# Loading every b tile as two halves on two DMA queues, in a batched matrix product on one Trainium2 core

## Chip, cores and metric

The kernel runs on one core of a Trainium2 chip. The metric is the device time of one execution in microseconds (us). Before the change three runs took 134.62, 134.85 and 134.93 us; their median is 134.85 us.

## The reference

1024 independent products of 64 x 64 matrices, in fp32:

```python
def setup_inputs():
    return {
        "a": np.random.randn(1024, 64, 64).astype(np.float32),
        "b": np.random.randn(1024, 64, 64).astype(np.float32),
    }

def reference(a, b):
    return np.matmul(a, b).astype(np.float32)
```

a, b and the result have 16.78 MB each, so 33.55 MB are read from HBM and 16.78 MB are written.

## The kernel before

**Tiles.** The batch is cut into 16 tiles of 64 matrices (index t) and 8 super-tiles of 128 (index s). One b tile is 1 MB in fp32, `[128 partitions, 16 groups, 128]`: a group is four matrices, and each partition takes two rows of one matrix, 512 B, from every group. One super-tile of a is 2 MB in four parts of 512 KB. GpSimd's queue loads three of them and casts them to bf16 on the way (`a_sb`), SyncE's queue loads the fourth in fp32 (`a_raw`). For the first super-tile all four parts come in fp32 on SyncE's and ScalarE's queues.

**Work on a tile.** VectorE regroups a super-tile into one bf16 tile (`regroup`, L108 and L111). TensorE transposes it (`transpose`, L120), two bf16 values taken as one fp32, and ScalarE copies the transposes out of PSUM (L123). VectorE spreads them into a block-diagonal operand (`spread`, four copies a tile, L133) and casts the b tile to bf16 (`cast`, L144; tile 0 is cast by ScalarE, tile 15 in quarters by both, L149 and L151). Then 64 matmuls (`multiply`, L189) and eight copies from PSUM into the fp32 output tile `o_sb` (L177): all eight on ScalarE for even tiles, six on ScalarE and two on VectorE for odd ones.

**Order.** The program is one straight sequence, and each engine and each DMA queue takes its own instructions in that order. At tile t the sequence is: spread and cast of tile t+1; the load of b tile t+3, whose buffer is that of tile t (three buffers); at some even tiles loads and transposes of a; the matmuls and evacuation of tile t; regrouping and transposes for a later super-tile; the store of tile t-1. Three super-tiles of a have buffers. The output has eight buffers, two of which also take the first super-tile of a.

**Queues.** A transfer is issued by an engine's instruction stream. SyncE does nothing but issue. ScalarE issues between its copies, so an issue takes its time, and one that waits holds the copies behind it. GpSimd issues the casting loads of a and the stores of tiles 0 to 13, 1 MB each (L166). The stores of the last two tiles go out in pieces on SyncE's and ScalarE's queues. In the profile q0 is GpSimd's queue, q1 SyncE's and q10 ScalarE's; 16 DMA engines serve all three.

**What the change touches.** `load_b` (L93 to L97) issues each b tile as one transfer, even tiles on SyncE's queue and odd ones on ScalarE's (L96). It is called three times ahead of the loop (L215, L216, L221) and once in each of the first 13 tiles (L235). Ahead of the loop, ScalarE has its two loads of a (L90) and a first copy that loads its table (L214) before these, and its two casts of the first super-tile (L105) after them.

Of the kernel before, what the change touches and what calls it, by code (L numbers as in the profile page):

```python
# [13 lines left out]
def kernel(  # L14
# [14 lines left out]
    nc = tc.nc  # L29
# [11 lines left out]
    b_v = b.rearrange("(t g h) (kp u) n -> t (h kp) g (u n)", h=4, g=16, u=2)  # L41
# [50 lines left out]

    def load_b(t):  # L93
        b_sb = b_pool.tile([128, 16, 128], fp32, name="b_sb")
        queue = nc.scalar if t % 2 else nc.sync
        queue.dma_start(out=b_sb[:], in_=b_v[t])  # L96
        b_tiles[t] = b_sb  # L97

    def regroup(s):
# [110 lines left out]
    with tc.manual_schedule():  # L210
        load_first_a()

        nc.vector.memset(warm[:, 0:1], 0.0)
        nc.scalar.copy(warm[:, 1:2], warm[:, 0:1])  # L214
        load_b(0)  # L215
        load_b(1)  # L216
        nc.vector.memset(bd_tiles[0][:], 0.0)  # L217
        make_identity(nc, identity)
        nc.gpsimd.memset(bd_tiles[1][:, 0], 0.0)
        load_a(1)  # L220
        load_b(2)  # L221
        nc.gpsimd.memset(bd_tiles[1][:, 1], 0.0)
        load_a(2)
# [63 lines left out]
```

## Time and profile before

| | |
|---|---|
| median of 3 runs (lowest to highest) | 134.85 us (134.62 to 134.93) |
| span of the profiled execution, first to last instruction | 133.4 us |
| median less that span | 1.4 us |
| busy: VectorE, ScalarE, TensorE, GpSimd | 94.6, 87.9, 64.4, 33.0 us |
| packets and MB: q0, q1, q10 | 6832 and 20.19, 7120 and 14.68, 5056 and 9.96 |
| HBM read and written | 33.55 and 16.78 MB |
| b loads, issue to landing | 14.8 to 25.2 us, median 16.8 |
| matmuls of tile 0 begin, of tile 15 end | 21.2 and 120.2 us |
| last store issued | 125.85 us |

The profile's execution has no time listed beside its span. The 1.4 us that the median of the timed runs lies above it is taken as what lies around the span.

Times in the views count from the start of the span. The page's slices cut the span into 40 equal parts, with the busy share in tenths. The DMA row is the mean busy share of the 16 DMA engines, and the row below it is what they moved in GB/s, a casting load counted by the bytes that it writes. The chain follows the work that ended last back from the last instruction. In a timeline the brackets hold the idle time of the engine before the instruction, and what ended it. A queue such as SPq or ACTq stands for the issuing instructions of SyncE or ScalarE.

### The profile page before, as it was taken

How to read it: one execution, taken by the hardware profiler on the slowest of the kernel's cores; microseconds unless marked ns; L12 is line 12 of the kernel's file. 1: busy time of each engine (PE TensorE's matmuls, PEld its weight loads, DVE VectorE, ACT ScalarE, POOL GpSimd, SP SyncE). 2: the span in 40 equal slices, each digit the busy share in tenths (PEclk: the TensorE clock that was granted, in tenths of full speed). 3: DMA queues.
4: the chain of work that ended last, by engine and by line, in shares of the span. 5: the costliest groups of instructions: out<-in, count | busy, mean ns of one | idle time of the engine just before them, and what ended most of it. 6: DMA issues, size and time to landing. Idle time of an engine off the chain costs nothing.

```text
span 133.4 us, 2837 instructions
## 1 busy us (share of the span) xinstructions
PE 64.4 (48%) x1152; PEld 61.1 (46%) x1152; DVE 94.6 (71%) x120; ACT 87.9 (66%) x161; POOL 33.0 (25%) x43
## 2 busy tenths in 40 slices
PE   0006406960089384289518970956197363970000
PEld 0006306950089274189418950945196363960000
DVE  5930399109998809995999699959999995987000
ACT  3225424999036998969595969696968969099600
POOL 8991000420090070341233021203020410300000
PEclk9999975797557999856985699599959955599555
DMA  3999999999999999999999999999999999999990
GB/s 77 371 329 311 307 311 281 284 306 325 327 312 401 316 320 333 399 384 397 311 281 375 406 389 351 304 316 390 394 396 387 396 392 391 402 405 398 382 319 18
DMA packets 19021, 45.01 MB, mean 337 GB/s; under 512 B 1088, under 2 KB 3136, under 8 KB 19008
## 3 DMA queue, kind: packets, MB, share of 16 engines
q0 software_dynamic: 6832, 20.19, 50.1%
q1 hardware_dynamic: 7120, 14.68, 30.4%
q10 hardware_dynamic: 5056, 9.96, 19.7%
q8 instruction: 9, 0.15, 0.4%
q14 instruction: 4, 0.03, 0.1%
HBM read 33.55 MB, written 16.78 MB: 377 GB/s over the span
## 4 chain that ended last, share of the span: by engine, by line
DMA 53%; DVE 15%; ACT 13%; PE 6%; issue 5%; SPq 2%; DVEq 0%; ACTq 0%
DMA b_sb<-in_b_dram 53%; ACT o_sb L177 9%; DVE at_bd L133 6%; PE o_ps L189 4%; DVE b_bf L144 4%; DVE o_sb L177 3%; PE at_ps L120 2%; ACT at_sb L123 2%; ACT b_bf L144 1%; SPq L90 1%; DVE a_bf L108 1%; SPq L96 1%; ACT b_bf L151 1%; DVE a_bf L111 0%; SPq L77 0%
## 5 line engine op out<-in xcount | busy, mean ns | idle before, releaser
L177 ACT COPY o_sb<-o_ps 64x512 f32<-64x512 f32 x106 | 61.5, 580 | 10.3 <-PE o_ps L189 9.0
L189 PEld LDWEIGHTS <-at_bd 128*128 128x128 bf16 x1024 | 42.3, 113 | 39.5 <-DVE b_bf L144 25.7
L189 PE MATMUL o_ps<-b_bf,at_bd 128*128 128x64 bf16 x960 | 42.6, 216 | 35.4 <-DVE b_bf L144 23.4
L133 DVE COPY at_bd<-at_sb 32x1024 f32<-32x1024 f32 x64 | 46.9, 733 | 14.1 <-ACT at_sb L123 11.8
L120 PE MATMUL at_ps<-identity,a_bf 128*128 128x128 f32 x128 | 21.2, 335 | 19.4 <-ACT a_bf L105 11.2
L166 POOL DMA_DIRECT2D out_dram<-o_sb x14 | 15.4, 1097 | 56.9 <-ACT at_sb L123 23.4
L120 PEld LDWEIGHTS at_ps<-identity,a_bf 128*128 128x128 f32 x128 | 19.3, 180 | 19.5 <-issue 19.5
L123 ACT COPY at_sb<-at_ps 128x512 f32<-128x512 f32 x32 | 17.5, 590 | 11.0 <-PE at_ps L120 7.8
L144 DVE CAST b_bf<-b_sb 128x2048 bf16<-128x2048 f32 x14 | 17.8, 1271 | 9.6 <-DMA b_sb<-in_b_dram 9.4
L73 POOL DMA_DIRECT2D a_sb<-in_a_dram x21 | 13.6, 662 | 26.4 <-DVE a_bf L108 19.4
L177 DVE COPY o_sb<-o_ps 64x512 f32<-64x512 f32 x14 | 9.7, 690 | 0.3
L108 DVE COPY a_bf<-a_sb 128x3072 bf16<-128x3072 bf16 x7 | 6.7, 950 | 0.0
L105 ACT CAST a_bf<-o_sb 128x1024 bf16<-128x1024 f32 x2 | 2.1, 1044 | 5.2 <-DMA o_sb<-in_a_dram 5.2
L111 DVE CAST a_bf<-a_raw 128x1024 bf16<-128x1024 f32 x7 | 4.8, 683 | 0.0
L144 ACT CAST b_bf<-b_sb 128x2048 bf16<-128x2048 f32 x1 | 1.9, 1900 | 3.9 <-DMA b_sb<-in_b_dram 3.9
L105 DVE CAST a_bf<-o_sb 128x1024 bf16<-128x1024 f32 x2 | 2.8, 1382 | 1.9 <-DMA o_sb<-in_a_dram 1.9
L217 DVE MEMSET at_bd<- 128x4096 f32 x1 | 3.5, 3472 | 0.8 <-issue 0.8
L177 DVE COPY o_sb<-at_ps 64x256 f32<-64x256 f32 x8 | 3.4, 422 | 0.5 <-PE at_ps L189 0.4
L151 ACT CAST b_bf<-b_sb 128x512 bf16<-128x512 f32 x2 | 1.1, 615 | 3.6 <-DMA b_sb<-in_b_dram 3.6
L177 ACT COPY o_sb<-at_ps 64x256 f32<-64x256 f32 x8 | 2.9, 366 | 0.1
L214 ACT ACT_TABLE_LOAD x1 | 1.3, 1283 | 2.3 <-issue 2.3
L189 PE MATMUL at_ps<-b_bf,at_bd 128*128 128x64 bf16 x64 | 2.0, 193 | 1.0 <-DVE at_bd L133 1.0
(12 smaller groups left out, 6.1 us busy)
## 6 DMA issues: line engine op xcount, KB each, us to landing
out_dram<-o_sb POOLq DMA_DIRECT2D x14, 1024.0 KB, 21.6
a_sb<-in_a_dram POOLq DMA_DIRECT2D x21, 256.0 KB, 16.4
a_raw<-in_a_dram SPq DMA_DIRECT2D x7, 512.0 KB, 18.7
o_sb<-in_a_dram SPq DMA_DIRECT2D x2, 512.0 KB, 5.9
o_sb<-in_a_dram ACTq DMA_DIRECT2D x2, 512.0 KB, 7.1
out_dram<-o_sb SPq DMA_DIRECT2D x2, 512.0 KB, 7.5
out_dram<-o_sb SPq DMA_DIRECT2D x2, 256.0 KB, 7.8
out_dram<-o_sb ACTq DMA_DIRECT2D x2, 256.0 KB, 5.5
```

The costliest lines, as they stand in the source:

```text
L73: nc.gpsimd.dma_start(out=a_sb[:, h, :, :].rearrange("p v k -> p (v k)"), in_=a_v[s, h], single_packet=True)
L105: copy(a_bf[:, :, h, :], a_sb[h].rearrange("p (v k) -> p v k", v=16))
L108: nc.vector.tensor_copy(a_bf[:, :, 0:3, :], cast_sb[:].rearrange("p h v k -> p v h k"))
L111: nc.vector.tensor_copy(a_bf[:, :, 3, :], raw[:])
L120: nc.tensor.transpose(at_ps[:, vo, :], a_cols[:, 4 * vo + 2 * j + wl, :], identity[:])
L123: nc.scalar.copy(at_tiles[s][:, j, :, wl, :, :], at_ps[:].rearrange("p vo (g mp) -> p g mp vo", mp=4),)
L133: nc.vector.tensor_copy(bd[rows, :, :, :, h, :].rearrange("p j g wl mo -> p j (g wl) mo"), at_tiles[t // 2][rows, :, half, :, :, :].rearrange(
L144: (nc.vector.tensor_copy if t else nc.scalar.copy)(b_bf[:], b_sb[:])
L166: store_queue(t, lo).dma_start(out=o_v[t, :, lo : lo + n, :], in_=o_sb[:, lo : lo + n].rearrange("p gh j wl n -> p (gh j wl n)"),)
L177: copies[2 * par + wl](dst, src)
L189: nc.tensor.matmul(o_ps[:, gl, g % 2, j, :], at_bd[:, j, g, :, u], b_bf[:, g, 64 * u : 64 * u + 64], start=(u == 0), stop=(u == 1),)
L217: nc.vector.memset(bd_tiles[0][:], 0.0)
```

## The change

Every b tile is loaded by two transfers, groups 0 to 7 on SyncE's queue and groups 8 to 15 on ScalarE's. The places in the program, the buffers and everything else stay.

```diff
     def load_b(t):
         b_sb = b_pool.tile([128, 16, 128], fp32, name="b_sb")
-        queue = nc.scalar if t % 2 else nc.sync
-        queue.dma_start(out=b_sb[:], in_=b_v[t])
+        nc.sync.dma_start(out=b_sb[:, 0:8, :], in_=b_v[t][:, 0:8, :])
+        nc.scalar.dma_start(out=b_sb[:, 8:16, :], in_=b_v[t][:, 8:16, :])
         b_tiles[t] = b_sb
```

## The prediction

> **What bounds the kernel now.** I read the page's slices, queues and chain first, then the windows, then the timelines of ScalarE and SyncE, then the packet records behind the DMA figures. The page first.
>
> ```profile
> DMA  3999999999999999999999999999999999999990
> GB/s 77 371 329 311 307 311 281 284 306 325 327 312 401 316 320 333 399 384 397 311 281 375 406 389 351 304 316 390 394 396 387 396 392 391 402 405 398 382 319 18
> ...
> q0 software_dynamic: 6832, 20.19, 50.1%
> q1 hardware_dynamic: 7120, 14.68, 30.4%
> q10 hardware_dynamic: 5056, 9.96, 19.7%
> ...
> DMA b_sb<-in_b_dram 53%; ACT o_sb L177 9%; DVE at_bd L133 6%; PE o_ps L189 4%; DVE b_bf L144 4%; DVE o_sb L177 3%; PE at_ps L120 2%; ACT at_sb L123 2%; ACT b_bf L144 1%; SPq L90 1%; DVE a_bf L108 1%; SPq L96 1%; ACT b_bf L151 1%; DVE a_bf L111 0%; SPq L77 0%
> ```
>
> The chain tempts: 53% of it is waiting for b tiles, the very transfers that the change touches. But the DMA row above it is full in every slice but the first and the last. The three queues (q0 is GpSimd's, q1 SyncE's, q10 ScalarE's) sum to 100.2% of the engines' time. A b tile takes 15 to 25 us to land because it shares a full pool, not because its own queue is slow. The page's GB/s count casting loads by what they write, half of what they read. Counted by what they read, the packet records give 398.8 GB/s on average from 4 to 128 us, and between 383 and 407 in every stretch of 4 us. So 49.45 of the 50.33 MB pass at one steady rate. What is left to win is the two ends.
>
> ```profile
> 4.00:20.00 16.00, 3.60 (x16) 3.38 (x17) 8.21 (x10) 5.15 (x7) 6.38 (x9) 0.94 1.07 329
> ...
> 100.00:116.00 16.00, 9.73 (x187) 9.13 (x186) 14.10 (x18) 11.47 (x22) 2.72 (x3) 0.71 1.03 393
> ...
> 124.00:128.00 4.00, 0.00 (x0) 0.00 (x0) 0.00 (x0) 1.76 (x5) 0.00 (x0) 0.50 1.07 379
> 128.00:129.00 1.00, 0.00 (x0) 0.00 (x0) 0.00 (x0) 0.00 (x0) 0.00 (x0) 0.50 1.04 362
> 129.00:130.00 1.00, 0.00 (x0) 0.00 (x0) 0.00 (x0) 0.00 (x0) 0.00 (x0) 0.50 0.64 223
> 130.00:131.00 1.00, 0.00 (x0) 0.00 (x0) 0.00 (x0) 0.00 (x0) 0.00 (x0) 0.50 0.17 58
> 131.00:132.00 1.00, 0.00 (x0) 0.00 (x0) 0.00 (x0) 0.00 (x0) 0.00 (x0) 0.50 0.05 17
> ```
>
> These are windows; the last two columns are the DMA share and GB/s, the columns before them PE, weight load, VectorE, ScalarE, GpSimd and the clock. The pool is full until 129 us and then runs out engine by engine until the last packet ends at 131.8. The 0.30 MB after 129 would take 0.8 us at 400 GB/s, so a perfectly even end would come 2.0 us earlier. That is the most that the order of the transfers can win at the end. VectorE is next: 14.1 us busy of 16 around 110 us.
>
> ```profile
> 19.29 1.90 ACT L144 CAST b_bf<-b_sb 128x2048 bf16<-128x2048 f32 x1 [3.87 <-DMA b_sb<-in_b_dram]
> ...
> 90.34 0.02 ACT L96 MOVE_SHAPE b_sb<-in_b_dram  x1 [0.52 <-DVE b_bf L144]
> 90.39 0.69 ACTq L96 DMA_DIRECT2D b_sb<-in_b_dram  x1
> 91.13 1.07 ACT L123 COPY at_sb<-at_ps 128x512 f32<-128x512 f32 x2 [0.77 <-issue]
> 92.09 4.74 ACT L177 COPY o_sb<-o_ps 64x512 f32<-64x512 f32 x8
> 97.81 3.55 ACT L177 COPY o_sb<-o_ps 64x512 f32<-64x512 f32 x6 [0.99 <-PE o_ps L189]
> ```
>
> This is ScalarE's timeline (start, length, what, idle time before it). An issue on this queue costs ScalarE 0.77 us, and it comes once per pair of tiles. Before an odd tile's evacuation ScalarE waits 0.99 us for the matmuls (1.27 to 1.38 in the neighbouring pairs).
>
> **The change part by part.** *Bytes and packets.* The bytes stay. Each half still has rows of 512 B, so I expect the same 2 KB packets: 512 per tile (85 ns each), as two times 256. There are 16 more transfers, 8 on each queue, and each leaves one 4-byte packet on every DMA engine. These last 22 ns on q1 and 9 ns on q10 (medians): 8 x 22 + 8 x 9 = 0.25 us per engine. The bounds are 0, since packets overlap (shares of 1.03 to 1.09), and 0.25; I take +0.1.
>
> *SyncE's issues.* It issues 16 halves for 8 tiles, and computes nothing. Its a_raw loads stand in the same order behind the b loads, with about the same bytes ahead.
>
> *ScalarE's issues.* 8 more. The price of one half is bounded by the 0.38 us of a 512-row store and the 0.77 above; I take 0.75, as its rows are of the b load's kind. 8 x 0.75 = 6.0 us in all. Two of them come at the start and six before the evacuations of the odd tiles 1 to 11. At tiles 5 to 11 they fall into the 0.99 to 1.38 us wait for the matmuls; at tiles 1 and 3 the evacuations follow their predecessors without a gap, so 1.5 us are uncovered, in a stretch where the pool is full. On the path that sets the end: 0. Without the cover each issue would delay the evacuations, then the stores, by 0.75 us.
>
> *Tile 0 comes earlier.* Tiles 0 and 1 now share the pool and land at 19.26 and 20.42. In the packet records the two had 534 packets through by 14.0 us, more than one tile. Halved on both queues, tile 0 lands near 14.9. ScalarE then casts it after its last at_sb copy (15.41), and the first matmul waits for the spread of tile 0, which ends at 15.45 + 4 x 0.71 = 18.3, instead of the cast at 21.2: up to 2.9 us earlier. Against this, SyncE shows what an issue behind a b tile can cost:
>
> ```profile
> 3.27 6.36 SPq L77 DMA_DIRECT2D a_raw<-in_a_dram  x1
> ...
> 10.85 11.30 SPq L77 DMA_DIRECT2D a_raw<-in_a_dram  x1
> ```
>
> The a_raw load behind tile 0 was held for 6.36 us, until 9.63, when 68 of the tile's 512 packets were through; the one behind tile 2 went when 70 were. So about 444 packets fit in a queue. ScalarE now issues halves of tiles 0, 1 and 2 ahead of its two casts of a (at 6.34 and 10.05): 512 packets stand before the third, which may be held until about 70 are through, near 10.7 (83 of tile 1 were at 11.0). Both casts would follow it (0.75 + 2 x 1.04), ending at 13.5 instead of 11.1, and the first matmul would still come at 20.7. So the computation starts 0.5 to 2.9 us earlier.
>
> *Where that goes.* Later, VectorE waits 9.4 us in five places for b tiles (4.0 of them at 50 us, for tile 4 behind three a_raw loads). A tile on two queues lands sooner, and these waits shrink. But the pool was full before, so earlier loads only push stores back, and the bill comes at the end: stores then stand queued while the last tiles are computed. The reserve is there. Tile 13's evacuation (109.7) reuses the buffer of tile 5, whose store landed at 96.3, so stores may slip 13 us.
>
> *Two load queues at once.* In stretches of 2 us with both load queues over 40 GB/s the pool moved 399.9 GB/s beside casting loads and 393.8 beside stores; with one of them 401.9 and 396.1. Both were active in 36 of 54. If the remaining third joined at 0.5% less: 0.005 x 0.33 x 124 = +0.2 us. The loads would end earlier in return: bounds 0 and, at the 1% that stretches of 1 us show, +0.4. I take +0.2.
>
> *The end.* Bounds 0 and -2.0. The first and the last DMA engine of one load land 2 to 3 us apart in the middle of the run too (47.41 and 50.09 for tile 4), so most of the uneven end stays; the last stores show 3.6 us (128.51 and 132.10). Only this excess of about 1 us can go, and I take -0.6.
>
> Sum: +0.1 + 0.2 - 0.6 = -0.3 us on a span of 133.4. The median of the runs is 1.4 us above that span, so 134.5.
>
> A rule of the Trainium skill speaks against the change. "DMA: Bandwidth & Descriptors", section Rules for kernel authors, says not to split a transfer into halves on two queues, as both run over the same 16 engines. Its section Anatomy of one DMA has a fixed 2.0 us per transfer; as an estimate by that page, 16 more would cost 32 us if nothing lay beside them. The rows here have the pool's share above 1.0 all along, so that fixed part lies beside other packets, and the sum by the rows stands.
>
> **The rivals.**
> - *ScalarE is held at its issues* (slower). As SyncE's a_raw was, a half issued behind unfinished halves can be held, and evacuations queue behind it. For: the holds of 6.36 and 11.30 us. Against: when tile 12 was issued (83.28), tile 10 had been moving since 76.3, so well over 68 packets were gone, and ScalarE's queue carries no a_raw. The eight completion counters are reused too: a GpSimd load waited 5.3 us for an unrelated store that had the same one. It decides once the last store issue (125.85) comes over 2 us later, as 1.48 MB, 3.7 us, are still queued then; beyond that the end moves one for one. Holds of 3 to 5 us past the cover: 135.5 to 138.
> - *The mix costs more* (slightly slower): 0.25 for the packets, 0.4 for the queues, no gain at the end, up to 0.3 more where SyncE's half waits for a_raw: 135.2 to 135.8.
> - *Nothing changes*: SyncE's queue moves 14.68 MB against 9.96, so the half there sets when a tile is complete, as late as before: 134.6 to 135.1.
> - *The end fills up* (faster): stores stand queued for all engines until the last moment, and the whole 2.0 us go, less 0 to 1.0 for the terms above: 132.9 to 133.9.
>
> **How the numbers follow.** What a measurement here can tell from no change is about 0.2%, 0.27 us. Forecast 0.40 (134.0 to 135.0; 0.26 of it faster, 0.14 same), end filled 0.12 (faster), nothing 0.10 (0.08 same, 0.02 slower), mix 0.15 (0.01 same, 0.14 slower), ScalarE held 0.23 (slower). Faster 0.38, same 0.23, slower 0.39. The range, 133.4 to 136.2, leaves out half of the filled end and half of the held case.
>
> **What would show it.** Right: q1 with 7248 packets and q10 with 5184 (128 more each, 16 engines by 8 transfers), with 14.68 and 9.96 MB as before; the DMA row full as before; the cast of tile 0 starting before 18 us; the 4.0 us wait for tile 4 shorter; the last matmul earlier than 118 us while the span moves by under 1 us. Wrong: a DMA slice below 9 in the middle, ScalarE's L96 issues lasting over 1 us, its wait for the matmuls replaced by waits at L96, or a rate below 395 GB/s.

## The result and the profile after

The changed kernel takes 147.63 us (median of four runs, 146.28 to 149.16), the kernel before 134.89 us beside it. The ratio is 1.0903, with a 95% interval of 1.0845 to 1.0962; the slowest run of the change, 149.16 us, counts as disturbed and is left out of the ratio. So the change is slower by 9%, and the forecast of 134.5 us with its range up to 136.2 was wrong. The profiled execution took 148.07 us, its span is 146.2 us.

The page of the changed kernel, in the rows that were shown of before:

```profile
DMA  3999999999999999999999999999999999997476
GB/s 87 386 272 231 235 232 282 332 324 308 319 255 382 272 261 400 382 277 273 391 366 263 303 350 350 382 344 356 339 373 306 382 374 298 374 351 273 152 260 215
DMA packets 43853, 45.01 MB, mean 308 GB/s; under 512 B 1344, under 2 KB 36160, under 8 KB 43840
...
q0 software_dynamic: 6832, 20.19, 45.5%
q1 hardware_dynamic: 19536, 14.68, 34.5%
q10 hardware_dynamic: 17472, 9.96, 23.6%
```

The bytes are the same to the last digit, but q1 has 19536 packets for 7120 and q10 17472 for 5056. The records say what they are: 32768 packets of 512 B, at a median of 27 ns, stand where 8192 packets of 2 KB at 85 ns stood. Four small ones take 108 ns. With their means (88 and 31 ns), the time that packets of b keep one DMA engine went from 45.2 to 62.7 us, while all other packets stayed at 89 to 90 us. The DMA row is still full for most of the span; a full row says that the engines have packets, not that they move 400 GB/s: from 4 to 124 us the packet records, with casting loads counted by what they read, give 399 GB/s before and 368 now.

Windows (last two columns: DMA share and GB/s), the first of the kernel before, the others of the changed kernel:

```profile
12.00:20.00 8.00, 2.80 (x14) 2.55 (x13) 4.36 (x7) 3.06 (x5) 0.00 (x0) 0.88 1.08 310
...
12.00:20.00 8.00, 0.00 (x0) 0.00 (x0) 0.00 (x0) 1.18 (x2) 0.00 (x0) 1.00 1.13 234
...
128.00:132.00 4.00, 3.29 (x63) 3.16 (x61) 3.04 (x5) 0.80 (x2) 1.20 (x1) 0.50 0.90 337
132.00:136.00 4.00, 2.20 (x43) 2.15 (x41) 2.14 (x5) 2.57 (x5) 0.15 (x1) 0.50 0.81 279
136.00:140.00 4.00, 1.62 (x31) 1.46 (x28) 3.33 (x8) 3.89 (x8) 0.00 (x0) 0.50 0.39 131
140.00:146.20 6.20, 0.00 (x0) 0.00 (x0) 0.00 (x0) 2.24 (x7) 0.00 (x0) 0.50 0.76 254
```

From 12 to 20 us the changed kernel moves 234 GB/s for 310 at a share of 1.13 for 1.08, and has no matmul yet. A part of this drop is only that more of its bytes are casting loads: counted by what they read it is 383 GB/s for 403. The last four rows show a pool that is no longer full: the last tiles are computed late, and their stores come when little else is left.

The loss can be cut in two at 124 us, by the bytes of the packet records. Before, 48.3 MB had passed by then, after the change 44.5. The 3.8 MB that are missing take 9.6 us at 399 GB/s. From 124 us to the last packet it took 7.8 us before and 21.0 us now, 13.2 us more: the 9.6 us, and 3.6 us of a pool that runs empty. The last packet ends at 145.0 for 131.8.

ScalarE's start shows the second thing that happened, first before, then in the changed kernel:

```profile
6.34 1.04 ACT L105 CAST a_bf<-o_sb 128x1024 bf16<-128x1024 f32 x1 [2.52 <-DMA o_sb<-in_a_dram]
...
6.39 12.39 ACTq L96 DMA_DIRECT2D b_sb<-in_b_dram  x1
18.82 1.99 ACT L105 CAST a_bf<-o_sb 128x1024 bf16<-128x1024 f32 x2 [15.03 <-issue]
```

The issue of its third half is held for 12.39 us, the casts of a wait behind it, and the first matmul starts at 28.1 us where it was 21.2. Which of the two makes the time, the packets or the hold, is what the first four runs ask.

### The profile page after: what moved, and what is told of

It is laid out like the page before. It is cut to its first block, busy times and chain, and to the rows that moved or that the text cites. A ratio compares the mean times of both kernels' runs of the same rounds, so it can differ in the third digit from the quotient of the medians.

```text
span 146.2 us, 2848 instructions
## 1 busy us (share of the span) xinstructions
PE 69.1 (47%) x1152; PEld 65.9 (45%) x1152; DVE 94.4 (65%) x120; ACT 87.9 (60%) x153; POOL 33.6 (23%) x43
## 3 DMA queue, kind: packets, MB, share of 16 engines
q1 hardware_dynamic: 19536, 14.68, 34.5%
q10 hardware_dynamic: 17472, 9.96, 23.6%
## 4 chain that ended last, share of the span: by engine, by line
DMA 31%; DVE 14%; ACT 7%; PE 3%; issue 2%; DVEq 0%; ACTq 0%
DMA b_sb<-in_b_dram 31%; DVE at_bd L133 7%; ACT o_sb L177 7%; DVE b_bf L144 3%; PE o_ps L189 3%; DVE o_sb L177 2%; DVE a_bf L108 1%; ACT b_bf L151 1%; DVE a_bf L111 0%; DVEq L144 0%; DVEq L133 0%; ACTq L166 0%
## 5 line engine op out<-in xcount | busy, mean ns | idle before, releaser
L189 PEld LDWEIGHTS <-at_bd 128*128 128x128 bf16 x1024 | 45.9, 118 | 42.3 <-DVE b_bf L144 29.8
L189 PE MATMUL o_ps<-b_bf,at_bd 128*128 128x64 bf16 x960 | 44.8, 221 | 37.7 <-DVE b_bf L144 21.9
L120 PE MATMUL at_ps<-identity,a_bf 128*128 128x128 f32 x128 | 22.3, 348 | 29.0 <-ACT a_bf L105 20.9
L120 PEld LDWEIGHTS at_ps<-identity,a_bf 128*128 128x128 f32 x128 | 20.4, 188 | 29.2 <-issue 29.2
L166 POOL DMA_DIRECT2D out_dram<-o_sb x14 | 16.5, 1177 | 66.0 <-ACT o_sb L177 21.4
L144 DVE CAST b_bf<-b_sb 128x2048 bf16<-128x2048 f32 x14 | 17.4, 1244 | 12.9 <-DMA b_sb<-in_b_dram 11.8
L73 POOL DMA_DIRECT2D a_sb<-in_a_dram x21 | 13.1, 638 | 31.9 <-DVE a_bf L108 30.7
L189 PE MATMUL at_ps<-b_bf,at_bd 128*128 128x64 bf16 x64 | 3.6, 240 | 1.8 <-ACT b_bf L151 1.8
```

The source lines that it names most:

```text
L73: nc.gpsimd.dma_start(out=a_sb[:, h, :, :].rearrange("p v k -> p (v k)"), in_=a_v[s, h], single_packet=True)
L120: nc.tensor.transpose(at_ps[:, vo, :], a_cols[:, 4 * vo + 2 * j + wl, :], identity[:])
L144: (nc.vector.tensor_copy if t else nc.scalar.copy)(b_bf[:], b_sb[:])
L166: store_queue(t, lo).dma_start(out=o_v[t, :, lo : lo + n, :], in_=o_sb[:, lo : lo + n].rearrange("p gh j wl n -> p (gh j wl n)"),)
L189: nc.tensor.matmul(o_ps[:, gl, g % 2, j, :], at_bd[:, j, g, :, u], b_bf[:, g, 64 * u : 64 * u + 64], start=(u == 0), stop=(u == 1),)
```

## The experiments

Theories, formed on the traces: **P**, the small packets make the time, wherever they are issued; **H**, ScalarE's hold at the start makes it. Each kernel ran beside the kernel before, whose median was 134.9 to 135.1 us in every group. In brackets stand the ratio to it and the ratio's 95% interval.

**Halves, but on one queue per tile.**

```diff
+        queue = nc.scalar if t % 2 else nc.sync
+        queue.dma_start(out=b_sb[:, 0:8, :], in_=b_v[t][:, 0:8, :])
+        queue.dma_start(out=b_sb[:, 8:16, :], in_=b_v[t][:, 8:16, :])
```

> Each b tile by two transfers of eight groups, but both on the tile's one queue by turns, as whole tiles were. Theory P (packets): what changed is the form of the packets, 512 B at 28 ns (112 ns for 2 KB) in place of 2 KB at 85 ns; 27 ns x 512 x 16 tiles / 16 engines = +13.8 us of each DMA engine's time, and a smaller share beside GpSimd's 4 KB packets. It expects 145 to 149 us. Theory H (hold): ScalarE is held 12.4 us at the start behind its third half, and every matmul comes 9 us later; here ScalarE has only the two halves of tile 1 before its casts, so it expects 134.5 to 138 us.

151.26 us (ratio 1.1206, 1.1148 to 1.1265). The casts of a start at 6.41 us as before the change, so the hold at the start is gone, and H misses by over 13 us. The first matmul is no earlier for it (29.7 us), as tile 0 lands late:

```profile
27.74 1.90 ACT L145 CAST b_bf<-b_sb 128x2048 bf16<-128x2048 f32 x1 [12.29 <-DMA b_sb<-in_b_dram]
```

So this run does not tell a late start from small packets; the pair after the next one does. It is even slower than the change, by 3.6 us, and above P's range. ScalarE is held for 11.95 us at its second half at 58.28 us and for 5.46 us at 94.05; what share of the 3.6 us that has was not tried apart.

**All halves on SyncE's queue.**

```diff
+        nc.sync.dma_start(out=b_sb[:, 0:8, :], in_=b_v[t][:, 0:8, :])
+        nc.sync.dma_start(out=b_sb[:, 8:16, :], in_=b_v[t][:, 8:16, :])
```

> All 32 halves on SyncE's queue, none on ScalarE's. Theory P expects 145 to 150 us, as the packets have the same 512 B, and perhaps a few us more, as one queue in place of two gets a still smaller share. Theory H expects 134.5 to 138 us, as ScalarE issues no b load and cannot be held.

148.24 us (1.0969, 1.0907 to 1.1031), as P expects. ScalarE issues no b load here and cannot be held, and yet the time is that of the change. A loss of this size needs no hold of ScalarE. It is not all of the packets' making, though: whole tiles on this one queue also cost 5.5 us (below). Its queues:

```profile
q1 hardware_dynamic: 36176, 23.07, 55.0%
...
q10 hardware_dynamic: 832, 1.57, 2.8%
```

**Whole tiles first, and halves first.**

```diff
+        if t < 3:            # the second kernel: t >= 3
+            queue = nc.scalar if t % 2 else nc.sync
+            queue.dma_start(out=b_sb[:], in_=b_v[t])
+        else:
+            (the two halves of the change)
```

> Tiles 0 to 2 whole and by turns as before the change, tiles 3 to 15 as halves on both queues. Theory P expects 13/16 of 13.8 = +11 us: 144 to 147 us. Theory H expects the start of before (first matmul at 21 us) and the rest within 2 us of it: 134.5 to 137 us.

> Tiles 0 to 2 as halves on both queues, tiles 3 to 15 whole and by turns. Theory P expects 3/16 of 13.8 = +2.6 us: 136.5 to 138.5 us, whatever ScalarE's hold at the start, as the DMA engines are full in that time. Theory H expects ScalarE held until about 18.8 us, the first matmul near 30 us, and 141 to 147 us.

145.07 us (1.0766, 1.0702 to 1.0831) with 13 tiles in halves, 138.33 us (1.0266, 1.0207 to 1.0324) with 3. Both are P's. The loss is 3.4 us for 3 tiles, 10.2 for 13 and 12.7 for 16: 1.15, 0.78 and 0.80 us a tile. P had 0.86, from 27 ns more for each 2 KB (112 less 85), 512 times a tile, over 16 engines; the means of the records give 17.5 / 16 = 1.09. The first kernel starts its matmuls when the kernel before does (21.21 us) and still loses 10.2 us. The second has the whole hold and its first matmul at 28.0 us, and loses 3.4 us, 0.8 more than the 2.6 us that P gave its packets:

```profile
6.67 12.07 ACTq L100 DMA_DIRECT2D b_sb<-in_b_dram  x1
18.78 1.99 ACT L109 CAST a_bf<-o_sb 128x1024 bf16<-128x1024 f32 x2 [14.97 <-issue]
```

**Does halving itself cost, at 2 KB packets?** Two kernels with b buffers for two tiles answer it, as their transfers have 16 groups:

```diff
+    b_v = b.rearrange("(t g h) (kp u) n -> t (h kp) g (u n)", h=4, g=32, u=2)
...
+        b_sb = b_pool.tile([128, 32, 128], fp32, name="b_sb")    # bufs=2, a pair of tiles
+        # first kernel: one tile on each queue
+        nc.sync.dma_start(out=b_sb[:, 0:16, :], in_=b_v[p][:, 0:16, :])
+        nc.scalar.dma_start(out=b_sb[:, 16:32, :], in_=b_v[p][:, 16:32, :])
+        # second kernel: half of each tile on each queue
+        nc.sync.dma_start(out=b_sb[:, 0:32:2, :], in_=b_v[p][:, 0:32:2, :])
+        nc.scalar.dma_start(out=b_sb[:, 1:32:2, :], in_=b_v[p][:, 1:32:2, :])
...
+            if half == 0 and t + 4 < n_t:
+                load_b(t // 2 + 2)
```

> b buffers for two tiles (32 groups, two of them in place of three for one tile); each pair is loaded by one transfer per tile, the first tile on SyncE's queue, the second on ScalarE's, 16 groups each. Theory P (only the 512 B packets cost time) expects 2 KB packets, 512 per tile, and 134.5 to 138 us; what it loses on before comes from the later loads, as a pair's buffer is free only after both casts. It is the baseline of the next one.

> The same buffers and places, but SyncE's transfer takes the even groups of both tiles and ScalarE's the odd ones: every tile comes in two halves on two queues, as in the change, and each transfer still has 16 groups. Theory P expects 2 KB packets and the time of the run above within 1 us. Theory Q (halving a tile over two queues costs time by itself: it is complete only when the slower queue is) expects it 4 us or more above the run above; a gain of over 1 us would say that halving itself helps, and that the packets ate the gain.

146.36 and 146.12 us (1.0853, 1.0769 to 1.0936, and 1.0815, 1.0764 to 1.0865). Both have 7120 and 5056 packets, as the kernel before. Halving over two queues made no difference that these runs can tell, and theory Q's 4 us did not come. A smaller cost could lie hidden, as both kernels wait for other things. The baseline itself missed its expectation by 8 us, for another reason: a pair's buffer is free only after the cast that was just issued, and ScalarE waits for that at its issue, ahead of the evacuations. From the waits of the first of the two:

```profile
PE o_ps L190 <- ACT o_sb L178: 36.0, 11, 7.4
...
ACT b_sb L96 <- DVE b_bf L145: 23.9, 6, 5.5
```

Here the pool ran at 400 GB/s until 96 us and then ran empty; a full-rate pool was not enough, because the loads were asked for late.

**All whole tiles on SyncE's queue.**

```diff
+        nc.sync.dma_start(out=b_sb[:], in_=b_v[t])
```

> All whole tiles on SyncE's queue, none on ScalarE's. Theory P expects 2 KB packets and 134 to 136.5 us: the pool is as full as before. If the load queues' share of the turns beside GpSimd's 4 KB packets matters, one queue has half the turns and the tiles come later: 137 us or more.

140.55 us (1.0412, 1.0369 to 1.0454), with 2 KB packets. The time is the one of the alternative that the expectation named, and the records fit it: from 12 to 20 us GpSimd's queue moved 259 GB/s and SyncE's 141, where the two load queues of before had 216 together. But a queue by itself is slower, too. Where GpSimd's queue had next to nothing, SyncE's alone reached 328 GB/s at a full share (last two columns), and its 2 KB packets took 104 ns at a median for 85 before. The two were not tried apart. VectorE waited 20.2 us for b, for 9.4 before:

```profile
88.00:92.00 4.00, 2.95 (x56) 2.95 (x57) 3.86 (x6) 1.01 (x2) 1.03 (x1) 0.63 1.02 328
```

```profile
DVE b_bf L143 <- DMA b_sb<-in_b_dram: 20.2, 6, 4.6
```

**Quarters.**

```diff
+        for q in range(4):
+            rows = slice(4 * q, 4 * q + 4)
+            (nc.scalar if q % 2 else nc.sync).dma_start(out=b_sb[:, rows, :], in_=b_v[t][:, rows, :])
```

> Each tile by four transfers of four groups, two on each queue. Theory P expects the same 512 B packets as the halves and 146 to 150 us. If the number of transfers or of issues is what costs, 32 more transfers double the loss: 155 us or more.

155.15 us (1.149, 1.1439 to 1.1541). The packets are those of the change, so P misses: more transfers cost as well. ScalarE spends from 5.52 to 26.62 us on its issues at the start:

```profile
5.52 21.10 ACTq L97 DMA_DIRECT2D b_sb<-in_b_dram  x5
26.66 1.99 ACT L106 CAST a_bf<-o_sb 128x1024 bf16<-128x1024 f32 x2 [22.84 <-DMA b_sb<-in_b_dram]
```

Each of these five issues waits for the landing of the transfer that used its completion counter before it: the landings at 16.27, 22.63 and 26.22 us are followed by issues at 16.29, 22.65 and 26.24. The pool falls to 83 GB/s between 32 and 36 us (packet records). This is the prediction's rival of the held ScalarE, with the reuse of the counters that it named.

**Five b buffers, for the change and for before.** After these, one question was whether late tiles (L) are a cost beside the rate (R) that earlier loads could hide.

```diff
-    b_pool = ctx.enter_context(tc.tile_pool(name="b_pool", bufs=B_AHEAD))
+    b_pool = ctx.enter_context(tc.tile_pool(name="b_pool", bufs=5))
...
-            if t + B_AHEAD < n_t:
-                load_b(t + B_AHEAD)
+            for tb in {0: [3], 1: [4, 5], 2: [6, 7]}.get(t, [t + 5]):
+                if tb < n_t:
+                    load_b(tb)
```

> The change with five b buffers in place of three: tile 3 is loaded at tile 0, tiles 4 and 5 at tile 1, 6 and 7 at tile 2, then tile t+5 at tile t. The rate of the 512 B packets stays, their lateness is hidden by earlier loads. Theory R (all of the loss is the pool's lower rate, 366 in place of 399 GB/s from 4 to 124 us) expects 146 to 148.5 us as before. Theory L (part of it is that small packets get a small share of the turns, tiles land late, the last ones are computed late and the pool runs empty at 287 GB/s from 124 us on) expects the empty end to fill: 50.3 MB at 366 GB/s are 137.5 us, with 6 us of start, end and what lies around the span 141 to 144.5 us.

> The same five buffers for the kernel before the change, whole tiles by turns. Control for the run above. The pool was full at 399 GB/s with three, so both theories expect 134 to 136 us; below 134 would say that before, too, tiles came late enough to cost time.

155.11 us (1.1486, 1.1456 to 1.1516) and 135.31 us (1.0038, 1.0014 to 1.0062). Whole tiles gain nothing from depth. Halves lose 7.5 us more, which neither theory expected. ScalarE is stuck at its issues in the middle of its work:

```profile
56.63 1.07 ACT L123 COPY at_sb<-at_ps 128x512 f32<-128x512 f32 x2 [9.34 <-issue]
...
93.20 1.07 ACT L123 COPY at_sb<-at_ps 128x512 f32<-128x512 f32 x2 [12.17 <-issue]
```

Most of both is again a reused completion counter. The issue at 92.78 us, ahead of the second row, comes when a half of SyncE's lands that was issued at 61.85 and had the same counter (92.72). Ahead of the first, ScalarE waits for one of its own halves (53.00), and the issue is then held for another 3.52 us.

So the run could not decide between L and R, and the pair after the next two repeats the question on SyncE's queue alone.

**Tile 2 loaded behind the first regrouping.**

```diff
-        load_b(2)
         nc.gpsimd.memset(bd_tiles[1][:, 1], 0.0)
         load_a(2)
         regroup(0)
+        load_b(2)
```

> The change with the load of tile 2 moved behind the first regrouping, so that ScalarE casts a before it issues its third half. Theory P with the hold free of cost expects 147 to 149 us, as the change. If the hold costs (the casting loads of GpSimd wait for the first super-tile and the pool ran at 307 to 339 GB/s from 24 to 36 us), 3 of 12 us there come back: 144 to 146 us.

147.29 us (1.0928, 1.0883 to 1.0973), as the change. But the hold was moved, not removed: the issue now takes 8.74 us at 10.32, between the casts and the copies of the transposes, and the first matmul comes at 25.0 us. The 3 us come earlier and are worth nothing.

**Fifteen groups and one.**

```diff
+        queue = nc.scalar if t % 2 else nc.sync
+        queue.dma_start(out=b_sb[:, 0:15, :], in_=b_v[t][:, 0:15, :])
+        queue.dma_start(out=b_sb[:, 15:16, :], in_=b_v[t][:, 15:16, :])
```

> Whole tiles by turns, but groups 0 to 14 in one transfer and group 15 in a second on the same queue. If halving as such makes the packets small, the 15 groups keep 2 KB packets and the time is 135 to 138 us. If only the whole tile of 16 groups gets them, nearly all packets have 512 B and the time is 146 to 152 us.

One run, 164.04 us. The packets are 512 B for all 16 groups:

```profile
q1 hardware_dynamic: 19536, 14.68, 31.1%
q10 hardware_dynamic: 17472, 9.96, 21.7%
```

Leaving one group out of the transfer is enough. In these runs, transfers of 16 groups over 128 partitions have 2 KB packets (the kernel before and the two pair kernels), and those of 15, 8, 4 and 1 groups have 512 B. The instruction records show a second mark: a MOVE_SHAPE stands ahead of each whole-tile issue (16 before, none in the change). In this layout the rows of neighbouring partitions lie one after the other in HBM, so a 2 KB packet may hold the rows of four partitions; the records do not say which rows a packet holds, nor why 16 groups get this form and 15 do not.

The time is above the range. ScalarE is held for 2.1 to 11.8 us at the second transfer of seven of the eight odd tiles; what that alone costs was not tried apart.

**Depth on SyncE's queue alone.** The edits are those of the two runs on SyncE's queue with the five buffers.

> All whole tiles on SyncE's queue with five b buffers. With three this took 140.6 us, although the packets have 2 KB: one load queue has fewer turns beside GpSimd's 4 KB packets, VectorE waited 20.2 us for b tiles. Theory L (lateness is a cost of its own, which earlier loads can hide) expects 135 to 137.5 us. Theory R (only the rate counts) expects 139 us or more, as the packets are the same.

> All halves on SyncE's queue with five b buffers, so that no issue can hold ScalarE. With three: 148.2 us. Both effects in the change: theory L expects lateness to be hidden and the rate of the 512 B packets to remain: the pool moves about 366 GB/s, 137.5 us, with start, end and what lies around the span 142 to 145 us. Theory R expects 147 to 149 us. 150 us or more would say that SyncE, held behind halves, also brings its a_raw loads late.

140.18 us (1.0379, 1.0362 to 1.0397) for 140.55 with three buffers, and 148.15 us (1.0962, 1.0915 to 1.1009) for 148.24. Depth hides nothing, and theory L falls in this form. With one queue, whole tiles and halves take 140.6 and 148.2 us at three buffers and 140.2 and 148.2 at five. So halves cost 7.7 and 8.0 us where no issue can hold ScalarE and both have the same queue. Apart from the packets only the number of transfers differs between them, so this is the cleanest price of the small packets here. It is less than the 12.7 us of the change. No run beat the kernel before.

## Why the prediction was wrong

*Bytes and packets.* This is the step that failed. It read "Each half still has rows of 512 B, so I expect the same 2 KB packets". The rows of 512 B and the packets of 2 KB stood side by side in the profile, and the question how four rows came into one packet was not asked. The term was +0.1 us for 256 completion packets. These came, and did cost 0.1 us an engine. But in place of the same 2 KB packets the records show 32768 of 512 B, and +17.5 us of every DMA engine's time. The median rose by 12.7 us. That it is less fits packets of several queues lying beside each other (shares of 1.13 for 1.08 in the windows above). About 8 us is what halves cost on SyncE's queue alone, where no issue can hold ScalarE. How the other 5 us divide between queue shares, later holds and waits at ScalarE's issues was not told apart.

*The pool.* The frame was right: the span follows the rate of the pool and its two ends. The rate was not a constant: 401 and 397 GB/s before (4 to 60 and 60 to 124 us) became 372 and 364, below the 395 that the prediction gave as a sign of being wrong.

*Two load queues at once.* +0.2 us was argued from stretches with one and two queues. The split between the queues moved far more than that. From 12 to 20 us the records show 299 GB/s for GpSimd's queue and 42 for each load queue; before, 186, and 119 and 97. A 4 KB packet of GpSimd's now meets 512 B in place of 2 KB. When GpSimd's queue was dry (28 to 32 us), the two load queues reached 307 GB/s, where the pool of before moved 396.

The Trainium skill, "DMA: Bandwidth & Descriptors", section Queues, rings and completion order, has each DMA engine take one packet from each queue in turn. As an estimate by that rule, with each packet record taken as one such packet, 4 KB against 512 B is 8 to 1; the records show 7.2 to 1 here, and 7.3 to 1 (341 and 47 GB/s) with all halves on SyncE's queue. The same page's Specifications give 512 B as the least transfer at line rate. The measurement differs: 512 B in 27 ns are 19 GB/s an engine, 2 KB in 85 ns are 24.

The Trainium skill's rule that the prediction cites, not to split a transfer, is written for halves of the partitions, and its fixed 2.0 us stand in a section on transfers that GpSimd issues. Here the halves are of groups, over all 128 partitions, on the two other queues. The rule pointed the right way, but the reason it gives, that both halves share the same engines, is not what cost the time here.

*ScalarE's issues.* Forecast at 0.75 us a half; they take 0.37 where nothing holds them, without a MOVE_SHAPE ahead. The third half was held as the prediction said, but until 18.8 us and not 10.7. It went when 786 of the 2048 packets ahead of it were through, 402 KB, where the prediction had 70 packets of 2 KB, 143 KB; and they drained at 42 GB/s beside the casting loads. The first matmul came 6.9 us later, and not 0.5 to 2.9 earlier.

*Tile 0* landed at 22.7 us, not at 14.9, through the same slow drain. *The end* grew emptier by 3.6 us; the forecast had -0.6.

*The rivals.* *The mix costs more* had the right kind of cause, with 0.25 us for the packets where the records show 17.5. The held ScalarE had the right sign and was real, with 12.4 us at the start and 4.7, 7.2 and 3.1 us later. The hold at the start did not set the time: three tiles with it, packets included, cost 3.4 us. The later ones may have a part in the 5 us that stay open, and ScalarE's waits at its issues are the likely cause in the quarters and with five buffers, where the packets are the same. How the 3.6 us at the end divide between late tiles and holds was not told apart.

## What to carry to other kernels

The packet size of a transfer can hang on its whole shape, so look up packets and bytes per packet of a transfer before cutting it, and check them first afterwards; here one group less made 2 KB into 512 B. Where the DMA engines are full, price a packet form by the time per byte and by what its queue gets beside the larger packets. On the queue of an engine that computes, count the issues that can be held, and what waits behind them. Taking all loads off that queue is no free cure: with whole tiles it cost 5.5 us here.

## What the runs showed of the hardware

- A 512 B packet took 27 ns and a 2 KB packet 85 ns at a median, 27% more per byte (39% by the means); that the size alone does it, and not something else in that form of transfer, was not tried apart.
- With 2 KB packets, one load queue alone moved 328 GB/s at 104 ns a packet, three queues together 400 at 85 ns. Moving all whole tiles to one queue cost 5.5 us, with the same packets.
- An issue on ScalarE's queue was held for 12.39 us until 786 of the 2048 packets ahead of it were through. In another run ScalarE stood still for 12.17 us, most of it until the transfer landed that had used the completion counter of its next issue.
- Five b buffers in place of three changed next to nothing for whole tiles by turns (0.4% slower) and on SyncE's queue, and cost 7.5 us where ScalarE issues halves.
